# Attention of layer 0: the five blocks of queries in the order 1, 2, 0, 3, 4 instead of 0, 1, 2, 3, 4

## The chip, the cores and the metric

The kernel runs on one core of a Trainium2 chip. The metric is the device time of one execution in microseconds (us). Three executions of the kernel before took 2100.63, 2105.58 and 2110.71 us; their median is 2105.58. The profile comes from an execution of its own, which took 2108.86 us.

The core's engines are named as in the profile: PE is TensorE's matrix work and PEld its weight loads, DVE is VectorE, ACT is ScalarE, POOL is GpSimd, SP issues DMA transfers. A matrix instruction is a MATMUL; a transpose is one too (against the identity matrix, called `ca` in the rows). TensorE's granted clock is 2.4 GHz (shown as 1.00) or 1.2 GHz (0.50).

## The reference, cut to what matters

The program is one step of a two-layer network over 640 tokens: 128 of a prompt and 512 of a sample. In layer 0 two groups of heads work side by side on one input projection, and one output projection takes both results:

```python
def block_attention(q, k, v):            # 8 query heads, 2 key heads, 64 wide
    def one_block(qblk):                 # 128 queries
        s = jnp.einsum('bqkgd,bskd->bkgqs', qblk, k).astype(F32) * scale
        p = jax.nn.softmax(s, axis=-1).astype(v.dtype)
        return jnp.einsum('bkgqs,bskd->bqkgd', p, v)
    o = lax.map(one_block, qb)
...
attn = block_attention(q, keys, vals)    # prompt: its own 128 keys; sample: 128 cached + 512 own
y_f, hf = ssd_chunked(xs, ...)           # a scan in chunks of 128 tokens, forward
y_b, hb = ssd_chunked(xs[:, ::-1], ...)  # and backward
out = jnp.einsum('bte,ed->btd', jnp.concatenate([attn, y], axis=-1), w_out)
```

A block of queries needs nothing of another block. The prompt's one block (block 0) sees 128 keys; each of the sample's four (1 to 4) sees 640.

## The kernel before, in words

The tokens stand in five blocks of 128: block 0 is the prompt, 1 to 4 the sample. Keys, values and queries of all five lie in SBUF when the stage begins; nothing of the attention is loaded in it.

`attention(b)` works through the eight heads in pairs (0 and 4, 1 and 5, ...). For each head TensorE makes the scores in PSUM (`psS`, L728: for a long block two halves of 320 keys, each from a high and a low part of the keys, so four matmuls; for block 0 two matmuls of 128). VectorE takes the row maximum (`nm`, L731) and scales it (L732), ScalarE makes the exponentials (`pe`, L734), TensorE transposes them (`pT`, L739: five transposes, or one for block 0; the fifth goes into free columns of `psS`), ScalarE and VectorE copy them out (`pts`, L742 and L744), and after every second head TensorE multiplies both with the values (`po`, L751). At the end of a block the sums of all heads are inverted and spread (L755 to L763), and the result is split into a high and a low part for the output projection (`mh`, `ml`, L768 and L769). There are two PSUM tiles for scores and one for transposes.

`ssd()` is the scan. It first makes decay factors (`sums`, L781) and the states carried from chunk to chunk (`states`, two directions: GpSimd's product `xde` at L803, TensorE's L807, VectorE's updates of `hT` at L823 and L825), and then for each chunk of 128 tokens a chain over all engines (`chunk`: L843, L863 with exponentials at L865, L875, for chunks 1 to 4 L882, then a norm over the row on VectorE, and the transposes of L706 into `mh` and `ml`).

Both are Python generators. The loop at L910 to L915 takes one head of attention and one step of the scan in turn: 40 heads against 37 steps, so the scan ends with the last block. Below it a scheduler lays the instructions into one fixed order for each engine by priority (order of writing) and by its own estimate of when an engine is free; every engine then runs its list in that order and waits where an input isn't ready. So both the order of writing and the scheduler's estimate set what stands behind what.

Of the kernel before, what the change touches and what calls it, by code (L numbers as in the profile page):

```python
# [83 lines left out]
def build(tc, I, O):  # L84
    with ExitStack() as ctx:
        _build(ctx, tc, I, O)


def _build(ctx, tc, I, O):
# [358 lines left out]
    with l0st as st:  # L448
# [242 lines left out]
        with ExitStack() as s1:  # L691
# [208 lines left out]
            def ssd():  # L900
                sums()
                for d in range(2):
                    steps_of(0, d)
                yield from states(0)
                yield from states(1)
                for b in range(5):
                    yield from chunk(b)
                    yield

            other = ssd()  # L910
            for b in range(5):
                for _ in attention(b):
                    next(other, None)
            for _ in other:
# [1055 lines left out]
```

## Time and profile before

| what | number |
|---|---|
| runs | 2100.63, 2105.58, 2110.71 us; median 2105.58 |
| profiled execution | 2108.86 us |
| its span in the profile | 2107.0 us |
| TensorE busy in the span | 1940.9 us (92%) |
| VectorE, ScalarE, GpSimd busy | 1433.5, 941.8, 563.4 us (68%, 45%, 27%) |
| mean granted clock of TensorE | 0.942 |
| the attention stage | 200.65 to 377.03 us |

The span is what the profiler saw from the first to the last instruction; the time of the execution is 1.9 us longer. "Busy" of TensorE counts from the start of a matmul to its modelled end, so where matmuls follow each other the distance of their starts says what one costs. A granted clock of 0.50 doubles that distance. Idle time is given with what ended it: "[1.36 <-POOL xde L803]" reads: idle for 1.36 us, until GpSimd's instruction of line 803 that wrote `xde`.

### The profile page before, as it was taken

Reading aid. Unit: us, or ns where it says so; the run is one execution under the profiler, and the core shown is the slowest. Engines: PE = TensorE matmul, PEld = TensorE weight load, DVE = VectorE, ACT = ScalarE, POOL = GpSimd, SP = SyncE. Lnnn points to the kernel's source line nnn. Section 1 sums busy time; section 2 is a strip of 40 time slices with the busy share of each in tenths; the row PEclk is TensorE's granted clock in tenths of the full one; section 3 lists DMA queues with packets and bytes.
Section 4 is the critical chain, followed back from the end, with each engine's and each line's share of the span. In section 5 each row is a group of like instructions: output and inputs, shape, how many; then the busy total and the mean of one; then the engine's idle time right before and its main releaser. Section 6 shows DMA issues by size and latency. Waiting matters only on the chain. (4 is left out here: it accounts for less than half of the span.)

```text
span 2107.0 us, 42812 instructions
## 1 busy us (share of the span) xinstructions
PE 1940.9 (92%) x17625; PEld 1767.9 (84%) x17625; DVE 1433.5 (68%) x2597; ACT 941.8 (45%) x1742; POOL 563.4 (27%) x515
## 2 busy tenths in 40 slices
PE   7999989999999999989999897877789899999998
PEld 6888677989999999968676886766679799999998
DVE  4474676458675757678585839889966777666675
ACT  4332445344433524446665343444463535344351
POOL 2111232001343426031144123313321025243330
PEclk8999899999999999989999988878879999999999
DMA  9764000522342424332377634435344422323221
GB/s 293 224 202 113 9 1 1 170 91 81 110 141 81 149 62 131 121 119 66 118 234 247 207 101 129 120 86 147 93 148 125 121 80 81 101 64 97 61 91 51
DMA packets 256406, 245.71 MB, mean 117 GB/s; under 512 B 27849, under 2 KB 217298, under 8 KB 256084
## 3 DMA queue, kind: packets, MB, share of 16 engines
q1 hardware_dynamic: 233076, 208.87, 32.9%
q0 software_dynamic: 5856, 21.01, 3.1%
q10 hardware_dynamic: 17280, 13.11, 2.0%
q8 instruction: 138, 2.26, 0.4%
q14 instruction: 56, 0.46, 0.1%
HBM read 203.76 MB, written 39.19 MB: 115 GB/s over the span
## 5 line engine op out<-in xcount | busy, mean ns | idle before, releaser
L979 DVE TENSOR_TENSOR ol<-wr,oh 128x512 fp32r<-128x512 f32 x344 | 304.7, 902 | 103.9 <-ACT oh L978 96.0
L978 ACT CAST oh<-wr 128x512 fp32r<-128x512 f32 x344 | 211.2, 620 | 312.4 <-PE d L1130 176.1
L1130 PE MATMUL d<-hid,oh 128*128 128x320 f32 x1312 | 292.5, 311 | 3.6 <-DVE hid L1028 2.1
L1130 PEld LDWEIGHTS d<-hid,oh 128*128 128x128 f32 x1312 | 221.6, 189 | 5.1 <-DVE hid L1028 3.3
L1130 PE MATMUL d<-hid,ol 128*128 128x320 f32 x656 | 203.8, 311 | 0.0
L443 DVE SCALAR_TENSOR_TENSOR x<-d,mod,x 128x128 f32<-128x128 f32 (+2 forms) x204 | 77.3, 433 | 142.6 <-PE d L1130 116.3
L1000 POOL TENSOR_TENSOR g<-wr 128x512 f32<-128x512 f32 x36 | 49.4, 1372 | 459.1 <-DMA wr<-in_ffn_w_up_dram 315.0
L1130 PEld LDWEIGHTS d<-hid,ol 128*128 128x128 f32 x656 | 124.3, 189 | 0.0
L401 PE MATMUL d<-hh,wh 128*128 128x320 f32 (+1 forms) x464 | 118.7, 328 | 3.9 <-ACT at L1404 1.8
L401 PE MATMUL d<-hl,wh 128*128 128x320 f32 (+1 forms) x464 | 114.4, 319 | 2.7 <-POOL hl L436 2.7
L401 PE MATMUL d<-hh,wl 128*128 128x320 f32 (+1 forms) x464 | 113.5, 316 | 0.4 <-DVE wl L388 0.4
L388 DVE TENSOR_TENSOR wl<-wr,wh 128x1024 fp32r<-128x1024 f32 (+1 forms) x57 | 72.3, 1269 | 56.8 <-ACT wh L386 56.4
L386 ACT CAST wh<-wr 128x1024 fp32r<-128x1024 f32 (+1 forms) x57 | 58.7, 1034 | 102.6 <-PE d L401 64.9
L401 PEld LDWEIGHTS d<-hh,wh 128*128 128x128 f32 (+1 forms) x464 | 79.1, 190 | 16.5 <-ACT at L1404 3.9
L401 PEld LDWEIGHTS d<-hl,wh 128*128 128x128 f32 (+1 forms) x464 | 79.3, 190 | 7.1 <-POOL hl L436 5.4
L1027 ACT CAST hid<-e 128x320 fp32r<-128x320 f32 x88 | 40.5, 460 | 97.9 <-DVE e L1045 97.4
L401 PEld LDWEIGHTS d<-hh,wl 128*128 128x128 f32 (+1 forms) x464 | 79.8, 190 | 2.1 <-DVE wl L388 1.1
L1553 PE MATMUL pS<-ar,ta 64*128 64x128 f32 x640 | 58.6, 325 | 21.8 <-POOL uv L1621 10.2
L1003 POOL TENSOR_TENSOR wr<-wr 128x512 f32<-128x512 f32 x36 | 52.7, 1468 | 84.3 <-DVE ol L979 32.9
L1553 PEld LDWEIGHTS pS<-ar,ta 64*128 64x128 f32 x640 | 51.2, 227 | 28.4 <-POOL ar L1540 12.4
L1005 POOL TENSOR_TENSOR wr<-wr 128x512 f32<-128x512 f32 x36 | 54.0, 1512 | 65.3 <-DVE ol L979 64.3
L1581 DVE TENSOR_TENSOR xt__11678<-ta 128x31 f32<-128x31 f32 (+15 forms) x155 | 67.3, 434 | 4.4 <-POOL ta L1569 0.2
(637 smaller groups left out, 5957.3 us busy)
## 6 DMA issues: line engine op xcount, KB each, us to landing
wt<-in_mod_w_dram SPq DMA_DIRECT2D x80, 512.0 KB, 4.4
wr<-in_ffn_w_gate_dram SPq DMA_DIRECT2D x44, 512.0 KB, 4.7
wr<-in_ffn_w_up_dram SPq DMA_DIRECT2D x44, 512.0 KB, 5.0
wr<-in_ffn_w_down_dram SPq DMA_DIRECT2D x44, 512.0 KB, 4.5
ta<-kbd SPq DMA_DIRECT2D x10, 1024.0 KB, 6.9
ar<-rkd SPq DMA_DIRECT2D x20, 512.0 KB, 6.8
wr<-in_ab_w_in_dram SPq DMA_DIRECT2D x16, 512.0 KB, 8.0
wt<-in_mod_w_dram SPq DMA_DIRECT2D x6, 1024.0 KB, 10.5
```

Source lines behind the costliest of these rows:

```text
L386: S.copy(wh, wr)
L388: V.tensor_sub(wl, wr, wh.bitcast(F32))
L401: T.matmul(ps[b][0:cn, 0:320], w[:, k, 0:cn], a[:, t0:t1], start=(k == 0 and i == 0), stop=(k == w.shape[1] - 1 and i == 2))
L443: V.scalar_tensor_tensor(out=x[:, k, c0:c1], in0=ps[b][:, c0 - 320 * b:c1 - 320 * b], scalar=mod[:, layer, v, gcol + k:gcol + k + 1], in1= ...
L978: S.copy(hi, src)
L979: V.tensor_tensor(out=lo, in0=src, in1=hi.bitcast(F32), op=ALU.subtract)
L1000: E.tensor_tensor(out=g3, in0=a11, in1=a21, op=ALU.add)
L1003: E.tensor_tensor(out=a11, in0=a11, in1=a21, op=ALU.add)
L1005: E.tensor_tensor(out=a12, in0=a12, in1=a11, op=ALU.add)
L1130: T.matmul(bank[:, 0:c1 - c0], p, q, start=i == 0 and z == 0, stop=i == n - 1 and z == 2)
L1553: T.matmul(pS[i][:, m], bk[r, g4 * 4 + m, :], ar[r, g4 * 4 + m], start=True, stop=True)
L1581: V.tensor_tensor(out=tv, in0=nu[:, j + 1:32, j:j + 1].to_broadcast([128, n, j + 1]), in1=wu[:, j:j + 1, 0:j + 1].to_broadcast([128, n, j ...
```

## The change

The loop over the blocks of queries takes them in another order; nothing else is written differently.

```diff
             other = ssd()
-            for b in range(5):
+            for b in (1, 2, 0, 3, 4):
                 for _ in attention(b):
                     next(other, None)
```

The scan's steps keep their order and their turns. Before, the eight heads of block 0 alternate with the eight steps of `states`; now the heads of block 1 do, and block 0 comes third, in turns 17 to 24, beside the end of chunk 1 and the most of chunk 2 as they are written. The scheduler then orders each engine's list anew. GpSimd's list is the same as before, and so is everything behind this stage.

TensorE where the stage begins, before. `psS` are scores (kh and kl the high and low part of a key group, qs the queries), `pg` the scan's results, `pT` transposes, `po` the products with the values; the last number is the shape that an instruction writes, x4 that four stand in a row:

```order
L728 MATMUL psS<-kh_208,qs 128x128
L728 MATMUL psS<-kl_210,qs 128x128
L781 MATMUL pg_2176<-dta,cb__207 128x40 x4
L781 MATMUL pg_2176<-dta,ca 128x40 x2
L794 MATMUL pg_2193<-ca,h_2191 64x128 x4
L728 MATMUL psS<-kh_209,qs 128x128
L728 MATMUL psS<-kl_211,qs 128x128
L739 MATMUL pT<-ca,pe 128x128
L728 MATMUL psS<-kh_208,qs 128x128
L728 MATMUL psS<-kl_210,qs 128x128
L807 MATMUL pg_2202<-xde,btok 64x256 x2
L739 MATMUL pT<-ca,pe 128x128
```

And with the change, at the same place:

```order
L728 MATMUL psS<-kh_208,qs 128x320
L728 MATMUL psS<-kl_210,qs 128x320
L728 MATMUL psS<-kh_208,qs 128x320
L728 MATMUL psS<-kl_210,qs 128x320
L781 MATMUL pg_2183<-dta,cb__207 128x40 x4
L781 MATMUL pg_2183<-dta,ca 128x40 x2
L794 MATMUL pg_2200<-ca,h_2198 64x128 x4
L728 MATMUL psS<-kh_209,qs 128x320
L728 MATMUL psS<-kl_211,qs 128x320
L728 MATMUL psS<-kh_209,qs 128x320
L728 MATMUL psS<-kl_211,qs 128x320
L739 MATMUL pT<-ca,pe 128x128 x4
```

The first heads' scores are now of a long block (two halves of 320), and the first product of the scan's states (L807) stands behind five transposes instead of one.

VectorE at the same place, before (maximum, factor, the first carried state `hT`, and the decay factors `decg` and `dde` that GpSimd's first `xde` needs):

```order
L731 TENSOR_REDUCE nm<-psS 128x1
L732 TENSOR_SCALAR nm<-nm,rq 128x1
L796 COPY hT<-pg_2193 128x256
L731 TENSOR_REDUCE nm<-psS 128x1
L732 TENSOR_SCALAR nm<-nm,rq 128x1
L784 COPY decg<-ex 64x40 x2
L785 TENSOR_TENSOR dde<-ex,dtt 128x80
L823 TENSOR_TENSOR hT<-hT,decg 128x256
```

With the change:

```order
L731 TENSOR_REDUCE nm<-psS 128x1
L796 COPY hT<-pg_2200 128x256
L732 TENSOR_SCALAR nm<-nm,rq 128x1
L731 TENSOR_REDUCE nm<-psS 128x1
L784 COPY decg<-ex 64x40 x2
L785 TENSOR_TENSOR dde<-ex,dtt 128x80
L732 TENSOR_SCALAR nm<-nm,rq 128x1
L823 TENSOR_TENSOR hT<-hT,decg 128x256
```

The copy of `hT` now stands ahead of the first head's factor, and `dde` behind the second head's maximum only.

TensorE with the change behind the state products of chunk 1 (L882), where the short block now runs; these rows stand ahead of the chunk's transposes (L706):

```order
L728 MATMUL psS<-kh_208,qs 128x128
L728 MATMUL psS<-kl_210,qs 128x128
L882 MATMUL pg_2914<-hT,bc 128x256
L882 MATMUL pg_2915<-hT,bc 128x256
L739 MATMUL pT<-ca,pe 128x128
L728 MATMUL psS<-kh_209,qs 128x128
L728 MATMUL psS<-kl_211,qs 128x128
L751 MATMUL po<-pts,vt 64x128
L739 MATMUL pT<-ca,pe 128x128
L728 MATMUL psS<-kh_208,qs 128x128
L728 MATMUL psS<-kl_210,qs 128x128
L751 MATMUL po<-pts,vt 64x128
```

Before, the same place held heads of a long block:

```order
L728 MATMUL psS<-kh_208,qs 128x320
L728 MATMUL psS<-kl_210,qs 128x320
L728 MATMUL psS<-kh_208,qs 128x320
L728 MATMUL psS<-kl_210,qs 128x320
L882 MATMUL pg_2848<-hT,bc 128x256
L882 MATMUL pg_2849<-hT,bc 128x256
L739 MATMUL pT<-ca,pe 128x128 x4
L739 MATMUL psS<-ca,pe 128x128
L751 MATMUL po<-pts,vt 64x128 x9
L728 MATMUL psS<-kh_209,qs 128x320
L728 MATMUL psS<-kl_211,qs 128x320
L739 MATMUL pT<-ca,pe 128x128 x4
```

There short heads with 128 keys stand now, with one transpose each, where heads with 640 keys and five transposes stood.

## Rows read from the trace of the kernel before

**Rows 1.** Stretches: length, busy PE, PEld, DVE, ACT, POOL (count), granted clock, DMA.

```profile
200.65:228.18 27.53, 24.73 (x112) 14.23 (x110) 14.84 (x41) 8.91 (x27) 10.05 (x10) 0.59 0.20 54
228.18:254.50 26.32, 24.25 (x206) 20.18 (x205) 16.96 (x49) 14.47 (x33) 5.91 (x5) 0.98 0.00 1
254.50:282.50 28.00, 25.17 (x204) 20.33 (x204) 20.56 (x56) 14.84 (x34) 9.51 (x8) 1.00 0.01 1
282.50:312.50 30.00, 26.04 (x230) 21.43 (x224) 21.35 (x55) 14.27 (x33) 9.93 (x7) 1.00 0.01 1
312.50:340.05 27.55, 24.44 (x194) 19.66 (x193) 18.80 (x51) 13.52 (x29) 9.42 (x7) 1.00 0.00 1
340.05:365.97 25.92, 23.67 (x194) 19.38 (x193) 17.60 (x54) 14.33 (x32) 2.53 (x2) 1.00 0.00 1
```

**Rows 2.** The same view, shorter stretches at the stage's start and end.

```profile
203.00:204.00 1.00, 0.27 (x2) 0.13 (x2) 0.96 (x5) 0.99 (x4) 0.00 (x0) 1.00 0.52 153
205.00:206.00 1.00, 0.00 (x0) 0.00 (x0) 0.56 (x3) 0.06 (x1) 1.00 (x1) 0.73 0.88 231
206.00:207.00 1.00, 0.90 (x4) 0.29 (x4) 0.00 (x0) 0.00 (x0) 1.00 (x2) 0.50 0.80 231
229.00:230.00 1.00, 1.00 (x6) 0.80 (x6) 1.00 (x7) 0.58 (x2) 0.00 (x0) 0.82 0.00 0
364.00:366.00 2.00, 1.27 (x10) 0.79 (x9) 1.60 (x8) 1.30 (x3) 0.00 (x0) 0.97 0.00 0
366.00:368.00 2.00, 2.00 (x16) 1.67 (x16) 0.35 (x1) 0.46 (x2) 0.00 (x0) 0.50 0.00 0
```

**Rows 3.** Timeline of PE at full clock: start us, us, what was done.

```profile
255.05 0.66 PE L739 MATMUL pT<-ca,pe 128*128 128x128 f32 x4
255.57 0.39 PE L728 MATMUL psS<-kh,qs 128*128 128x320 f32 x1
256.33 0.49 PE L843 MATMUL pg<-bc 64*128 64x128 f32 x2
256.75 0.43 PE L751 MATMUL po<-pts,vt 128*64 128x128 f32 x2
257.11 0.41 PE L728 MATMUL psS<-kh,qs 128*128 128x320 f32 x1
...
348.29 1.30 PE L751 MATMUL po<-pts,vt 128*64 128x128 f32 x18
349.53 1.55 PE L875 MATMUL pg<-xdt,e 128*128 128x64 f32 x12
```

**Rows 4.** Timeline of PE in the stage's first part, at half clock.

```profile
206.10 1.12 PE L807 MATMUL pg<-xde,btok 128*64 128x256 f32 x4 [1.36 <-POOL xde L803]
207.15 0.48 PE L739 MATMUL pT<-ca,pe 128*128 128x128 f32 x1
207.56 0.69 PE L751 MATMUL po<-pts,vt 128*64 128x128 f32 x2
208.18 0.48 PE L728 MATMUL psS<-kh,qs 128*128 128x128 f32 x1
208.59 0.69 PE L751 MATMUL po<-pts,vt 128*64 128x128 f32 x2
...
226.81 0.64 PE L728 MATMUL psS<-kh,qs 128*128 128x320 f32 x1
```

**Rows 5.** Timeline of DVE where the stage begins.

```profile
201.81 1.23 DVE L388 TENSOR_TENSOR wl<-wr,wh 128x1024 fp32r<-128x1024 f32 x1 [0.17 <-ACT wh L386]
...
203.28 0.21 DVE L732 TENSOR_SCALAR nm<-nm,rq 128x1 f32<-128x1 f32 x1
203.41 0.41 DVE L796 COPY hT<-pg 128x256 f32<-128x256 f32 x1
```

**Rows 6.** Groups in the stage: shape, count, busy us, mean ns, idle before them.

```profile
L734 ACT ACTIVATE pe<-psS,nm,rq 128x640 f32<-128x640 f32 x32 | 28.3, 885 | 28.6 <-PE psS L728 18.4 <-DVE nm L732 4.9 <-DVE rq_w L121 2.5
...
L731 DVE TENSOR_REDUCE nm<-psS 128x1 f32<-128x640 f32 x32 | 26.2, 819 | 6.3 <-PE psS L728 6.3
```

## The prediction

> **What bounds the kernel now.** I read the page first, for the span (2107.0 us) and its row of the granted clock. The change touches one stage only, the attention of layer 0 with the scan that runs beside it, from 200.65 to 377.03 us; behind it the instructions are the same on every engine and in the same order. So I cut that stage with the windows view at the places where the scan passes from one part to the next: first the states (sums and carried states, up to the first matmul of L843), then the five chunks (each up to the transposes of L706) [rows 1]. What is to be seen: in the five chunk phases TensorE is busy 24.25, 25.17, 26.04, 24.44 and 23.67 us of 26.32, 28.00, 30.00, 27.55 and 25.92. That is 123.57 of 137.79, and 14.2 us idle; VectorE has 95.3 busy. TensorE is the engine that sets the pace there, at a full clock. The states phase is another thing: 27.53 us, 24.73 of them busy, but at a mean granted clock of 0.59. Taken at full clock its work is about 24.73 x 0.59 = 14.6 us. So some 12.9 us of this phase are idle time and half clock. The finer windows show how it came: TensorE is busy 0.27 us between 203 and 204 and not at all between 205 and 206, the granted clock falls to 0.50 (1.2 GHz) there and is back at 1.00 (2.4 GHz) only after 229 [rows 2]. All eight heads of block 0, the prompt's short one, run inside that stretch.
>
> **What the change moves.** Nothing is added or removed; the same instructions stand in another order, and GpSimd's order is unchanged. A head of a long block costs TensorE, by the distance of starts at full clock [rows 3]: five transposes 255.05 to 255.57, 0.52; the four score matmuls to 256.33, 0.76; the ten matmuls on the values, two heads together 0.36 + 1.24, so 0.80 a head. Sum 2.08 us. A head of the short block at half clock [rows 4]: transpose 0.41, score matmuls 2 x 0.41, values 0.62: 1.85, so 0.92 at full clock.
>
> Counted in TensorE's order, the states phase had 8 short heads and the score matmuls of one long head; it gets 7 long heads. The five chunk phases had 6, 6.75, 6, 6 and 6 long heads (in quarters, by score matmuls issued); now they have 8.75, then 1.25 and the 8 short ones, then 4, 3.75 and 7. What follows the last chunk's transposes is the same as before, with the same quarter head to go, so it costs the same.
>
> States phase: 14.6 - 8 x 0.92 - 0.76 + 7 x 2.08 = 21.0 us of work at full clock. On top come three terms. First, idle time at the start. VectorE is held by the weight split until about 203.04, then takes 0.82 for the first long maximum, 0.41 for a copy that now stands ahead of the factor, and 0.21 for the factor; ScalarE's exponential takes 0.89 [rows 5, 6]. So the first transpose can start near 205.5; TensorE has issued two heads' scores and the state sums by about 204.1 (with two short heads' it was done by 203.3: it is busy 0.27 us after 203 [rows 2]), which leaves 1.4 idle. Then the first state matmul waits for GpSimd's product, as it did for 1.36 us before [rows 4]; its input comes after the second long maximum, about 1 us later than before, but five transposes stand ahead of the wait: 1.0 idle. For the rest of the phase I take 1.5, half of a chunk phase's mean idle time (14.2/5 = 2.8). Together 3.9; between 2.4, the start alone, and 5.2 with a whole phase's. Second, the clock: the thin stretch at the start is still there, so I expect the fall still to happen near 206. But from about 207 on long heads follow each other. In the trace the clock came back within 3 us of the first long head's score matmuls (they begin at 226.81) [rows 2, 4]; if it does so again, some 3 us of busy time run at half clock, 1.5 lost. Bounds: 0 if it never falls, and about 18 if all work after the start runs at half clock. Sum: 21.0 + 3.9 + 1.5 = 26.4, against 27.53: a gain of 1.1.
>
> Chunk phases: 6 long heads leave (30.75 to 24.75), 8 short ones come: -6 x 2.08 + 8 x 0.92 = -5.1. Two terms stand against it, both in the phase of chunk 1, where the short heads now run. Its TensorE work becomes 25.17 - 5.5 x 2.08 + 8 x 0.92 = 21.1; with the smallest idle time of a phase (2.07) it could end in 23.2. But the chunk is a chain over all engines, and no chunk phase of the trace is shorter than 25.92, so between 0 and 2.7 us of it are idle beyond the usual: I take 1.5. And TensorE is thin again behind that chunk's state products, while VectorE does the row norm of the chunk. How the clock takes such a stretch can be seen at the end of the stage: with 1.27 of 2 us busy between 364 and 366 it falls to 0.50 [rows 2]. It came back soon there, since dense work followed. One such fall costs about half of 3 us of busy work, 1.5; the bounds are 0 and about 10, what the states phase lost (24.73 - 14.6 = 10.1). So the chunk phases change by -5.1 + 1.5 + 1.5 = -2.1.
>
> Total: -1.1 - 2.1 = -3.2. The profiled execution took 2108.86 us (span 2107.0), so 2105.7 on its base. The median of the three runs is 2105.58, 3.3 below it, and I state the time against the median: 2102.4.
>
> A rule that speaks against this change: the Trainium skill, "TensorE: Matmul & The Clock Gate", section "HAM oscillation — how this bites in real kernels", says that a loop whose bursts are parted by waits pays for the return of the clock again in every turn, and that it is better to keep the engine fed throughout. By it a thin stretch moved to the middle pays there a second time, on top of the one that the start still has; that is the second rival below, priced from rows.
>
> **Rivals.**
> *The clock holds in both places.* For it: with long heads TensorE has more to do in the first microseconds (eight long score matmuls instead of four short), and the thin stretch of chunk 1 has, by the windows, neighbours that are dense. Against it: the 2.4 us of idle time at the start follow from VectorE's order, not from the clock. Then the states phase takes 21.0 + 2.4 = 23.4 (-4.1), with the start's idle time alone, and the chunk phases -5.1 + 0.8, with half of the chain's idle time: -8.4, about 2097.
> *The half clock moves with the short block.* For it: the short heads ran at half clock for 24 us because they give TensorE too little, and they are as small in the middle. Against it: there they run beside a chunk's dense matmuls and not beside the states. The start still loses 1.5, and the middle loses 9 to 10 instead of 1.5: -3.2 + 8 = +5, about 2108 to 2111: no change that can be told.
> *The clock doesn't come back at the start, slower.* One mechanism, in the states phase: after the fall near 206 long heads at half clock wait often enough, for GpSimd's products and the one transpose bank, that the clock stays down until the chunk's matmuls. Price: 21.0 - 2.5 = 18.5 us of work at half clock, +18.5 in place of +1.5: -3.2 + 17 = +14, about 2117 to 2120. It decides from the point where the clock is still at 0.50 by the fourth long head (about 217). Against it: 229 to 230, where the very first long heads brought it back.
> That the change doesn't move the work is ruled out by the orders above: the long block stands first on TensorE and VectorE.
>
> **How the numbers follow.** The forecast has 0.55 (its own range 2098 to 2107), the clock that holds 0.20, the half clock in the middle 0.14, the slow start 0.11. I take 0.5%, about 10.5 us, as what a measurement tells from no change: the three runs span 2100.63 to 2110.71. Faster by more (below 2095.0) is the low half of the first rival and a rest of the forecast's tail: 0.15. Slower by more (above 2116.1) is nearly all of the third rival: 0.10. The rest, 0.75, is within. The range 2092 to 2113 holds the forecast, most of the first rival and the second, and leaves out the third and the far end of the first.
>
> **What would show it.** In the profile after: the states phase with 7 long heads in 25 to 28 us, its granted clock above 0.8 and no longer 0.59; a fall near 206 that ends before 213; the phase of chunk 1 shorter than 28.0 us, 23 to 26, with a dip of the clock of a few us behind its state products; chunk 0 and chunk 4 each longer than before by about two heads (4 to 6 us) and one head (2 us), chunk 3 shorter by about 4.5. Wrong would be a states phase at 0.6 again, or chunk phases whose sum doesn't fall below 137.8 us, which would mean that the chunks' chain and not TensorE set their length.

## The result, and the profile after

The changed kernel takes 2117.30 us (median of 6 runs, 2114.86 to 2119.52), the kernel before 2104.84 (6 runs, 2100.63 to 2110.71): a ratio of 1.0057, 95% interval [1.0043, 1.0071]. I forecast 2102.4 with a range of 2092 to 2113. The change makes the kernel slower, by 12.5 us, and the prediction was wrong in its sign.

The profiled execution has a span of 2117.2 us against 2107.0. The stage begins 0.36 us later and takes 10.8 us more; all that lies behind it takes 1 us less. These are its stretches, cut at the same places as [rows 1] and with the same columns (length, busy PE, PEld, DVE, ACT, POOL, granted clock, DMA): states, chunks 0 to 4, and what follows the last chunk's transposes.

```profile
201.01:226.59 25.58, 22.91 (x165) 16.17 (x163) 17.82 (x42) 11.44 (x21) 10.03 (x10) 0.87 0.22 58
226.59:260.30 33.71, 29.64 (x258) 24.87 (x259) 21.46 (x58) 17.58 (x39) 6.02 (x5) 1.00 0.00 1
260.30:289.30 29.00, 27.36 (x181) 21.21 (x177) 19.92 (x58) 13.12 (x42) 9.74 (x7) 0.79 0.00 1
289.30:318.20 28.90, 23.87 (x160) 18.80 (x158) 19.34 (x51) 12.49 (x30) 9.48 (x7) 0.85 0.00 1
318.20:350.45 32.25, 27.44 (x173) 22.19 (x172) 16.58 (x42) 9.80 (x22) 10.05 (x7) 0.79 0.00 1
350.45:377.59 27.14, 24.77 (x198) 20.32 (x198) 18.81 (x56) 15.01 (x34) 2.54 (x2) 1.00 0.01 2
377.59:388.19 10.60, 8.20 (x67) 6.55 (x65) 2.76 (x8) 3.41 (x8) 0.00 (x0) 0.76 0.66 230
```

Read each row in three parts: work (busy PE times clock: what the busy time would be at full clock), half clock (busy PE times one minus clock: what the lower clock adds) and idle (length less busy PE). The states phase did what was forecast: 25.58 us in place of 27.53, at a clock of 0.87 in place of 0.59. The five chunk phases grew from 137.8 to 151.0 us, and by their parts:

| five chunk phases, us | before | after | difference | forecast |
|---|---|---|---|---|
| work | 123.1 | 118.0 | -5.1 | -5.1 |
| idle | 14.2 | 17.9 | +3.7 | +1.5 |
| half clock | 0.5 | 15.1 | +14.6 | +1.5 |

The work left the chunk phases nearly as counted. (A row's mean clock is only a rough divider. With the busy time summed inside the half-clock stretches themselves, work comes to 122.9 and 116.6 us and half clock to 0.6 and 16.5; idle time is the same.) The clock took back about three times as much. Shorter stretches of the same view show where: TensorE runs at 1.2 GHz from about 277 to 294 us, from 315 to 322, from 332 to 339, and for 3 us from 346. Before, no chunk phase but the first microsecond of chunk 0 had any of that.

```profile
276.00:278.00 2.00, 1.17 (x6) 0.97 (x6) 1.93 (x6) 0.49 (x2) 0.79 (x2) 0.82 0.03 8
277.30:294.40 17.10, 16.97 (x66) 11.51 (x66) 9.05 (x39) 7.62 (x28) 3.57 (x3) 0.50 0.00 1
294.00:296.00 2.00, 2.00 (x18) 1.80 (x15) 1.23 (x4) 0.58 (x1) 0.00 (x0) 0.91 0.00 0
314.00:316.00 2.00, 0.12 (x1) 0.12 (x2) 1.79 (x12) 1.15 (x3) 0.00 (x0) 0.71 0.00 0
314.85:321.68 6.83, 5.80 (x31) 4.54 (x31) 3.49 (x17) 3.53 (x8) 1.04 (x1) 0.50 0.00 0
331.90:338.75 6.85, 6.85 (x40) 5.84 (x38) 0.69 (x1) 0.00 (x0) 2.04 (x2) 0.50 0.00 0
344.00:346.00 2.00, 1.43 (x7) 1.01 (x8) 1.76 (x13) 1.73 (x5) 0.00 (x0) 0.89 0.00 0
345.57:349.00 3.43, 3.41 (x13) 2.62 (x13) 1.05 (x7) 0.75 (x2) 0.00 (x0) 0.50 0.00 0
```

Half of the busy time of such a stretch is what its clock cost: 8.5, 2.9, 3.4 and 1.7 us, 16.5 together. The first of these stretches is the short heads'. TensorE's timeline reads there as it did in the states phase before [rows 4]: transposes, scores and values of a short head at half clock, 1.4 to 1.5 us from head to head.

```profile
280.38 0.48 PE L739 MATMUL pT<-ca,pe 128*128 128x128 f32 x1
280.51 0.46 PE L728 MATMUL psS<-kh,qs 128*128 128x128 f32 x1
280.76 0.41 PE L728 MATMUL psS<-kl,qs 128*128 128x128 f32 x1
281.21 0.69 PE L751 MATMUL po<-pts,vt 128*64 128x128 f32 x2
```

The other three have no short head near them. They stand in the phases of chunks 2 and 3, which have 4 and 3.75 long heads in TensorE's list where there were 6 and 6. Rows of the timeline from the norm of chunk 2 (the first row) and from chunk 3 show what TensorE does there (the brackets give idle time of the engine and what ended it; most rows between are left out):

```profile
315.88 1.12 PE L739 MATMUL pT<-ca,pe 128*128 128x128 f32 x4 [2.19 <-ACT pe L734]
...
324.91 0.68 DVE L866 TENSOR_TENSOR e<-e,gm 128x512 f32<-128x512 f32 x1
325.23 4.42 POOL L834 TENSOR_TENSOR am<-cb__207,dta 128x1024 f32<-128x1024 f32 x2 [5.74 <-PE pg L863]
325.81 4.99 DVE L866 TENSOR_TENSOR e<-e,gm 128x512 f32<-128x512 f32 x3
330.25 5.17 PE L875 MATMUL pg<-xdt,e 128*128 128x64 f32 x30 [1.39 <-DVE e L866]
335.46 0.69 DVE L876 TENSOR_TENSOR ys<-pg,ys 128x512 f32<-128x512 f32 x1 [4.13 <-PE pg L875]
340.62 0.82 DVE L731 TENSOR_REDUCE nm<-psS 128x1 f32<-128x640 f32 x1
342.08 0.69 DVE L891 TENSOR_TENSOR ys<-ys,zs 128x512 f32<-128x512 f32 x1 [0.63 <-POOL ys L888]
342.69 0.21 DVE L732 TENSOR_SCALAR nm<-nm,rq 128x1 f32<-128x1 f32 x1
342.81 0.63 ACT L894 ACTIVATE sc__3422<-ys 128x512 f32<-128x512 f32 x1 [14.57 <-DVE ys L891]
343.43 0.86 ACT L734 ACTIVATE pe<-psS,nm,rq 128x640 f32<-128x640 f32 x1
344.44 0.66 PE L739 MATMUL pT<-ca,pe 128*128 128x128 f32 x4 [3.28 <-ACT pe L734]
```

Two kinds of wait are seen. At 330.25 the y products (L875) wait 1.39 us for `e`; the clock falls behind it, and the thirty products take 5.17 us. At 315.88 and 344.44 the transposes of a head wait 2.19 and 3.28 us for its exponential (L734) while the chunk does its row norm, and the clock falls in the first of these waits and behind the second. The norm stands ahead of that head in two lists: VectorE has the head's maximum (L731) by 341.44, but then waits 0.63 us for GpSimd's sum and multiplies (L891) before it makes the head's factor (L732, 342.69), and ScalarE squares (L894) before the exponential. ScalarE's idle time of 14.57 us ahead of that square is not the length of this hold-up: until 340.62 VectorE hadn't begun the maximum of that head's scores, so for most of it there was no exponential to make. Before, ScalarE's list of this chunk had two heads' exponentials between the chunk's own last one (L865) and that square; now it has none. The groups of the stage show the same shift, against [rows 6]: the long exponentials cost the same (883 against 885 ns), but their idle time is now 11.4 us for VectorE's factor in place of 4.9, and 6.5 for scores in place of 18.4.

```profile
L734 ACT ACTIVATE pe<-psS,nm,rq 128x640 f32<-128x640 f32 x32 | 28.2, 883 | 22.4 <-DVE nm L732 11.4 <-PE psS L728 6.5 <-DVE rq_w L121 1.9
...
L731 DVE TENSOR_REDUCE nm<-psS 128x1 f32<-128x640 f32 x32 | 26.3, 821 | 8.6 <-PE psS L728 8.2
```

### The profile page after: what moved, and what is told of

It is laid out like the page before. It is cut to its first block, busy times and chain, and to the rows that moved or that the text cites. A ratio compares the mean times of both kernels' runs of the same rounds, so it can differ in the third digit from the quotient of the medians.

```text
span 2117.2 us, 42810 instructions
## 1 busy us (share of the span) xinstructions
PE 1948.1 (92%) x17625; PEld 1778.0 (84%) x17625; DVE 1437.9 (68%) x2597; ACT 941.1 (44%) x1742; POOL 565.7 (27%) x515
## 5 line engine op out<-in xcount | busy, mean ns | idle before, releaser
L978 ACT CAST oh<-wr 128x512 fp32r<-128x512 f32 x344 | 211.3, 620 | 310.3 <-PE d L1130 175.2
L1553 PEld LDWEIGHTS pS<-ar,ta 64*128 64x128 f32 x640 | 48.9, 216 | 30.7 <-POOL ar L1540 12.9
```

What stands on the lines that cost most here:

```text
L978: S.copy(hi, src)
L1553: T.matmul(pS[i][:, m], bk[r, g4 * 4 + m, :], ar[r, g4 * 4 + m], start=True, stop=True)
```

## The experiments

Two theories. *Short heads*: a run of short heads gives TensorE too little and the half clock moves with it. *Heads run ahead*: attention gets ahead of the scan (8.75 long heads beside chunk 0, short ones beside chunk 1), so chunks 2 and 3 keep four heads each, too few to cover the waits in the chunk's own steps. (The expectations of the first four runs set a *clock theory*, the first of these, against a *chain theory*: the scan's chain over all engines sets the length of a phase. The second theory came out of that one.) The table gathers all runs: long heads (+ short ones, s) beside chunks 0 to 4 in TensorE's list, then from the profile the stage (first scores to the last block's normalising product, L765), its idle time and half clock by the reading above, over seven stretches cut at each chunk's first L843 matmul (the before and after rows so differ a little from those above), and the ratio of times to the kernel before.

| kernel | heads beside chunks 0 to 4 | stage | idle | half clock | ratio [95% interval] |
|---|---|---|---|---|---|
| before | 6, 6.75, 6, 6, 6.25 | 177.1 | 19.2 | 13.4 | 1 |
| after | 8.75, 1.25+8s, 4, 3.75, 7.25 | 187.9 | 23.0 | 20.3 | 1.0057 [1.0043, 1.0071] |
| fill_before | as before | 174.4 | 19.1 | 6.3 | 0.9999 [0.9988, 1.0010] |
| fill_after | 8.75, 0.25+6s, 3.5+2s, 6.25, 6.25 | 187.9 | 20.9 | 16.6 | 1.0053 [1.0032, 1.0074] |
| o10234 | 2+8s, 4.5, 6.25, 6, 6.25 | 180.0 | 22.1 | 11.8 | 1.0012 [0.9997, 1.0028] |
| pace_after | 9, 2+8s, 4.75, 6.25, 3 | 175.2 | 20.2 | 10.9 | 1.0003 [0.9986, 1.0021] |
| lead_before | 8, 8, 4.5, 4, 6.5 | 202.4 | 25.8 | 29.9 | 1.0097 [1.0075, 1.0119] |
| spread | 6+2s, 7.75, 3.75+2s, 4.75+2s, 3.75 | 172.9 | 17.1 | 10.8 | 0.9983 [0.9970, 0.9995] |
| fill_mid | 8.75, 1.25+8s, 4.25, 4.25, 6.5 | 197.8 | 20.8 | 26.0 | 1.0112 [1.0090, 1.0133] |
| o12340 | 8.75, 6, 6, 4.25+1.5s, 6.5s | 170.1 | 18.8 | 7.8 | 0.9987 [0.9970, 1.0003] |
| amwait_after | 8, 1.75+8s, 4, 4.75, 6.5 | 204.1 | 30.4 | 30.0 | 1.0128 [1.0107, 1.0149] |
| amwait_before | 6, 6, 6.75, 4.75, 7.5 | 198.0 | 30.7 | 24.9 | 1.0110 [1.0092, 1.0128] |
| even | 7+1s, 4.5+1s, 4.5+2s, 5+1s, 5+1s | 189.9 | 18.7 | 21.7 | 1.0037 [1.0024, 1.0049] |
| amwait_even | 7+1s, 4.25+1s, 5.25+2s, 4.5+1s, 5+1s | 189.3 | 22.7 | 17.9 | 1.0071 [1.0054, 1.0089] |
| norm_after | 8.75, 1.25+8s, 4, 5, 6 | 184.3 | 23.2 | 16.4 | 1.0063 [1.0039, 1.0087] |
| even_last | 6.5, 6, 6, 6, 0.5+8s | 177.7 | 21.2 | 13.4 | 1.0014 [1.0000, 1.0028] |
| dveadd_after | 8.75, 0.75+8s, 3.5, 5, 7 | 197.2 | 21.0 | 30.6 | 1.0096 [1.0074, 1.0118] |
| dveadd_before | 6, 6, 6.5, 5.25, 7.25 | 171.7 | 18.0 | 5.8 | 0.9986 [0.9970, 1.0001] |

Before and after have 144.5 and 144.7 us of work by this reading, so all of the 10.8 us is half clock (+6.9) and idle time (+3.8). In spread, even and amwait_even the out-projection's first matmuls lie inside the stage. The stage is read from one execution of each kernel, the ratio from all of them: the profiled execution of even took 2119.22 us and that of o10234 2115.42, the longest of each (medians 2112.56 and 2107.42), so their stages may be longer than usual. From the stage's end to the end of the span the profiled executions take 1719.7 (lead_before) to 1733.3 us (fill_before). So stages are compared by their traces and times by the ratios.

**fill_before, fill_after.** Four dummy matmuls behind the scores of each short head:

```diff
+                    if b == 0:
+                        for f_ in range(4):
+                            T.matmul(psS[:, 1, 0:320], qs[:, h, 128:256], kh[h // 4][:, 128:448], start=f_ == 0, stop=f_ == 3)
```

> The kernel before, and in each of the eight heads of block 0 four matmuls of 320 columns more, into the unused half of that head's score tile; nobody reads them. Order otherwise unchanged. Clock theory (the short heads give TensorE too little, and the half clock is what costs): the states phase keeps 2.4 GHz or gets it back early, its work is 14.6 + 8 x 0.65 = 19.8 us at full clock with about 3 to 4 idle, so 23 to 25 us in place of 27.5: the kernel becomes 2 to 4 us faster although it does more, about 2101. Chain theory (the states' chain over GpSimd, TensorE and VectorE sets the pace, the clock is only a mark of it): 27.5 us or more, 0 to 5 us slower.

> The changed kernel with the same four matmuls more in each head of block 0, which stands third. Clock theory: the 17 us of half clock beside chunk 1 and 2 go, the added 5 us are paid back: 5 to 9 us faster than the changed kernel, 2108 to 2112. Chain theory: a chunk takes its 27 to 30 us whatever the clock: within 3 us of the changed kernel, 2114 to 2120, unless the scheduler spreads the long heads otherwise (by its order the phases get about 7, 8.75, 0 with 6 short, 4.25 with 2 short, 6.25 and 6.25 long heads; then the phase of chunk 3, which has 6.25 in place of 3.75, gets shorter than its 32 us by chain theory alone).

In the order of before the half clock at the start ended near 215 us instead of 229. The stage has 7.1 us of half clock less, 6.0 of them there, and the dummies' own work took 4.5. The states phase took 27.07 us (27.53 before), not the 23 to 25 of the clock theory, and the time didn't change. In the changed order they bought nothing: the clock was down from 277 to 297 all the same, and chunk 2 took 36.6 us at 0.70.

**o10234.** The short block second instead of third:

```diff
-            for b in (1, 2, 0, 3, 4):
+            for b in (1, 0, 2, 3, 4):
```

> Blocks in the order 1, 0, 2, 3, 4: long heads beside the states, the short block beside chunk 0. Long heads by phase: 7; 2 with 8 short; 4.5; 6.25; 6; 6.25. Clock theory: the states phase as in the changed kernel (25.6 us), the half clock once, for 15 to 20 us beside chunk 0, and then as before: 2108 to 2112. Chain theory: chunk 0 with 2 long and 8 short heads takes its 24 to 27 us as before with 6, chunk 1 with 4.5 takes 28, the others as before; so what the states phase gains (2 us) is all: 2103 to 2107.

The loss is nearly gone, though the short heads again stand in a run in the middle; the median, 2107.42, lies just between the two ranges. Beside them the clock was down from 250 to 264 us, but that fall stands at the end of a wait of 3.36 us for an exponential.

**pace_after.** The changed order, with the scan's steps given out by the weight of the heads:

```diff
-                for _ in attention(b):
-                    next(other, None)
+                for i_, _ in enumerate(attention(b)):
+                    for _ in range(int(b > 0 or i_ % 4 == 3) + (b > 1 and i_ == 3)):
+                        next(other, None)
```

> The changed order of blocks, but the scan takes a step only after every fourth short head, and two steps after the fourth head of blocks 2, 3 and 4, so that its 37 steps go with the long heads. Long heads by phase: 7; 9; 2 with 8 short; 4.75; 6.25; 3. Clock theory: the short heads still stand together beside chunk 1, half clock for 17 us: 2114 to 2119. Chain theory: chunk 3 with 6.25 heads in place of 3.75 no longer stalls (27.5 us in place of 32.3), but the last chunk has 3 heads in place of 7 and the end waits for its chain: 2110 to 2116.

With the same order of blocks the slowdown is gone (2105.36 us, below both ranges). The short heads still lose the clock (281 to 291 us, 10 us in place of 17), but chunks 2 and 3 lose it only for 3.4 us each. The edit changed both, so it doesn't say which of them counts for how much.

**lead_before.** The order of before, with no short head outside the states phase, but the scan held back in blocks 1 and 2 and doubled in block 3:

```diff
+            turns = (1,) * 8 + (1, 0, 1, 0, 1, 1, 0, 1) + (1, 1, 0, 1, 1, 0, 1, 1) + (2, 2, 2, 2, 2, 2, 1, 1) + (1,) * 8
...
-                for _ in attention(b):
-                    next(other, None)
+                for i_, _ in enumerate(attention(b)):
+                    for _ in range(turns[b * 8 + i_]):
+                        next(other, None)
```

> Order 0, 1, 2, 3, 4 as before, but the scan's steps are held back by some heads of blocks 1 and 2 and given out two at a time in block 3, so that the chunk phases have about 8, 8, 4.5, 4 and 6.5 long heads, as uneven as in the changed kernel, and no short head stands outside the states phase. Theory 'heads run ahead' (a chunk with only four long heads beside it leaves TensorE waiting in the chunk's own steps, which stretches the phase and lets the clock fall): chunks 2 and 3 not below 27.5 us each, with a mean granted clock under 0.90 in them, stage 183 to 187 us against 177.1, time 2111 to 2115. Theory 'short heads' (only the run of short heads in the middle costs): the clock stays above 0.97 in chunks 2 and 3, they shrink by about two heads to 24 to 26 us, chunks 0 and 1 grow by as much, stage 176 to 179, time 2103 to 2108.

This tells the theories apart: a loss comes without a short head outside the states phase, and a larger one than either theory gave (2125.85 us). These are the stretches of chunks 0 to 4; those of chunks 2 and 3 have 4.5 and 4 heads and are hardly shorter than those with 8 (33.3 and 32.4 us against 33.9 and 33.4).

```profile
228.87:262.81 33.94, 31.12 (x262) 25.74 (x261) 22.13 (x58) 17.92 (x42) 6.88 (x5) 0.93 0.00 1
262.81:296.18 33.37, 29.04 (x215) 23.45 (x214) 20.56 (x58) 15.69 (x36) 9.23 (x7) 0.95 0.01 1
296.18:329.52 33.34, 27.76 (x195) 22.88 (x194) 19.68 (x50) 12.20 (x31) 9.23 (x8) 0.85 0.00 1
329.52:361.87 32.35, 27.15 (x156) 20.67 (x155) 17.04 (x44) 9.79 (x22) 9.66 (x7) 0.75 0.00 1
361.87:390.50 28.63, 25.79 (x172) 21.23 (x171) 15.75 (x48) 11.55 (x27) 2.55 (x2) 0.80 0.00 1
```

TensorE's longest waits are of the same two kinds, for `e` and for an exponential at the row norm, and behind each of these the clock falls:

```profile
308.39 1.08 PE L875 MATMUL pg<-xdt,e 128*128 128x64 f32 x4 [2.22 <-DVE e L866]
324.30 0.66 PE L739 MATMUL pT<-ca,pe 128*128 128x128 f32 x4 [2.91 <-ACT pe L734]
...
340.22 4.53 PE L875 MATMUL pg<-xdt,e 128*128 128x64 f32 x30 [2.53 <-DVE e L866]
```

**spread.** The short heads in pairs in the middle of each long block (their sums on the values go to the free half of their score bank and are copied out; the carried states `hT` get 8 buffers in place of 9; the scan takes one step more between the two heads of a pair):

```diff
...
+            short = attention(0)
+            for b in range(1, 5):
+                for i_, _ in enumerate(attention(b)):
+                    next(other, None)
+                    if i_ == 3:
+                        next(short)
+                        next(other, None)
+                        next(short)
...
```

> The short block's heads in pairs in the middle of each long block (blocks 1, 2, 3, 4), their sums on the values in the free half of their score bank and copied out; no run of short heads anywhere. Theory 'short heads': with no run of them the clock loses only the fall at the start (about 3 us of busy time) and little at the end: 144 us of work at full clock, 19 us idle and 3 to 5 us by the clock, stage 166 to 170 us, time 2095 to 2099. Theory 'heads run ahead': the phases of chunks 2 to 4 have only 4 to 5 long heads beside them, so at least two of them show a clock under 0.90, and the stage takes 175 to 181 us, time 2103 to 2110.

Faster than the kernel before by 0.17% [0.05, 0.30], and so than both; less than the theory of short heads gave, and a little better than the other. Of chunks 2 to 4 one had a clock under 0.90 (0.88), where the second theory wanted two.

**fill_mid.** Dummies in the thin phases, in the changed order: four of 320 columns ahead of the transposes of each head of block 3, eight ahead of the y products of chunks 2 and 3.

```diff
+                    if b == 3:
+                        for f_ in range(4):
+                            T.matmul(pT[:, 0:320], qs[:, h, 128:256], kh[h // 4][:, 128:448], start=f_ == 0, stop=f_ == 3)
...
+                if b in (2, 3):
+                    for f_ in range(8):
+                        T.matmul(pY[:, 0:320], qs[:, 0, 128:256], kh[0][:, 128:448], start=f_ == 0, stop=f_ == 7)
```

> The changed order with dummy matmuls (their results are overwritten) where TensorE waits in chunks 2 and 3: four of 320 columns ahead of the transposes of each head of block 3, eight ahead of the y products of chunks 2 and 3, together 48, about 7 us at full clock. If the half clock is what makes these phases long: clock above 0.95 in chunks 2 and 3, the two together 53 to 57 us against 61.2, time 2110 to 2114. If the chain of waits through VectorE, ScalarE and GpSimd makes them long and the clock only follows: the two together 61 us or more, time 2117 to 2124.

Chunks 2 and 3 took 69.9 us together in place of 61 and the clock was no better:

```profile
287.60:323.76 36.16, 32.64 (x183) 26.01 (x182) 19.22 (x50) 12.27 (x29) 9.99 (x7) 0.74 0.00 1
323.76:357.51 33.75, 30.59 (x201) 25.50 (x200) 17.35 (x45) 11.26 (x26) 9.82 (x7) 0.80 0.00 1
```

No wait for an exponential over 1.3 us is left in these two phases. But TensorE still waits for `e` behind the dummies, 2.00 and 1.70 us (the y products are L881 here):

```profile
301.40 5.56 PE L881 MATMUL pg<-xdt,e 128*128 128x64 f32 x30 [2.00 <-DVE e L869]
...
334.34 4.48 PE L881 MATMUL pg<-xdt,e 128*128 128x64 f32 x30 [1.70 <-DVE e L869]
```

The clock falls behind each of these waits, and the time, 2127.72 us, is above both ranges. Here the dummies did not keep the clock up, and their work came on top.

**o12340.** The short block last:

```diff
-            for b in (1, 2, 0, 3, 4):
+            for b in (1, 2, 3, 4, 0):
```

> Order 1, 2, 3, 4, 0: the short block last, beside the last chunk. Chunks 0 to 3 have 8.75, 6, 6 and 4.25 long heads, the last chunk 6.5 short ones. Theory 'heads run ahead': only chunk 3 is thin, nothing comes behind the short heads but the out-projection: stage 168 to 173 us, time 2097 to 2101. Theory 'short heads': chunk 4 runs at half clock, 0.6 or below, and takes 26 us or more; stage 176 to 180, time 2104 to 2109.

The stage is the shortest of all, as the theory of heads that run ahead had it; the time, 2101.14, lies at the edge of its range, and its interval includes no change. The last chunk ran at 0.86, not at the 0.6 of the theory of short heads.

**amwait_after, amwait_before, even, amwait_even.** In the first two GpSimd's table for the next chunk takes the buffer of `e` and is written behind the y products, so it can't run beside VectorE's L866; even is built as spread, with single short heads after the second and sixth head of each long block and one step of the scan more after the fourth and eighth; the last has both.

```diff
-                am = ams[b, d] = wk.tile([128, 8, 128], F32, name="am", tag="am")
+                am = ams[b, d] = wk.tile([128, 8, 128], F32, name="am", tag="e")
...
-                    if b < 4:
-                        steps_of(b + 1, d)
                     yield
...
                 V.tensor_tensor(out=ys, in0=pY.rearrange("p (h d) -> p h d", h=8), in1=ys, op=ALU.add)
+                if b < 4:
+                    for d in range(2):
+                        steps_of(b + 1, d)
                 yield
```

> The changed order; GpSimd's decay table am of the next chunk takes the buffer of VectorE's product e, so it can only be written when the y products have read e, and no longer runs beside the product that makes e. Phases of 7, 8, 1.75 and 8 short, 4, 4.75, 6.5 heads, nearly as in the changed kernel. Theory 'the wait for e' (in a phase with few heads nothing on TensorE covers the wait of the y products for e, and the clock falls behind it): the three products in chunk 3 take 2.1 us and not 5.0, the wait of 1.4 us is gone, chunks 2 and 3 under 29 us each, time 2107 to 2112. Theory 'the wait at the row norm' (the heads' transposes that wait 2 to 3 us for an exponential queued behind the chunk's norm make the clock fall): those waits and the half clock behind them stay, time 2114 to 2119.

> The same shared buffer in the order 0, 1, 2, 3, 4. TensorE waited only 0.4 us in all for e there, so by both theories nothing to be gained: 2102 to 2107, unless the table now comes late for the next chunk (then chunk phases longer by 1 to 2 us each, 2107 to 2112).

> As the kernel with the short heads in pairs, but one short head at a time, after the second and the sixth head of each long block, so that the phases have about 6 + 2 short, 7 + 1, 4.5 + 1, 4.5 + 2, 5 + 1 and 5 + 1 short heads. If what costs is unevenness: no chunk phase over 31 us, fewer falls of the clock, 2095 to 2100. If phases with 4.5 long heads cost the clock whatever stands beside them: two of them at a clock under 0.90, 2101 to 2107.

> Both: short heads one at a time, and the shared buffer. If the wait for e is what makes thin phases lose the clock: 2092 to 2098; if the wait at the row norm does: as the even kernel alone, within 3 us of it.

L866 did become fast and the waits for `e` went. But the table now ran on GpSimd ahead of the sum (here L889) that the row norm waits for, and the heads' exponentials behind the norm came later still. VectorE's row and TensorE's two longest waits in amwait_after:

```profile
339.00 1.29 DVE L866 TENSOR_TENSOR e<-e,gm 128x512 f32<-128x512 f32 x2 [1.52 <-ACT e L865]
```

```profile
321.02 1.11 PE L739 MATMUL pT<-ca,pe 128*128 128x128 f32 x4 [6.76 <-ACT pe L734]
...
354.57 1.11 PE L739 MATMUL pT<-ca,pe 128*128 128x128 f32 x4 [5.14 <-ACT pe L734]
```

So this is no clean test of the wait for `e`; it shows that six heads a phase (amwait_before) are no cover for waits as long as these (up to 6.56 us there). All four medians, 2131.80, 2126.66, 2112.56 and 2120.07 us, lie above every range that was stated for them. And even was slower, not faster: with five long heads or fewer in four phases, chunk 3 took 43.5 us at a clock of 0.62 in its profiled execution.

**norm_after.** The row norm one step of the scan later:

```diff
+                yield
                 V.tensor_mul(ysf, ysf, zs[:, b, :])
...
                     yield from chunk(b)
-                    yield
```

> The changed order; the row norm of a chunk is written one step of the scan later, together with the next chunk's first step. In ScalarE's list of chunk 3 one more exponential stands ahead of the norm's square; chunk 2's list is as it was. Heads by phase 7, 8.75, 1.25 and 8 short, 4, 5, 6. Theory 'the wait at the row norm': the stall of 14.6 us of ScalarE in chunk 3 and TensorE's wait of 3.3 us are at most half of that, one fall of the clock less, chunk 3 29 us or less though it has one head more, time 2108 to 2113. Theory 'the wait for e': the wait of 1.4 us and the half clock behind it stay, chunk 3 32 us or more, time 2114 to 2119.

The fall at 346 us went, the wait fell from 3.28 to 2.27 us, and chunk 3 took 32.0 us with 1.25 heads more. But ScalarE's idle time was still 14.17 us, though an exponential and not the norm's square now stood behind it, and the wait for `e` (1.38 us) and the fall behind it stayed:

```profile
329.93 5.15 PE L875 MATMUL pg<-xdt,e 128*128 128x64 f32 x30 [1.38 <-DVE e L866]
...
342.09 0.89 ACT L734 ACTIVATE pe<-psS,nm,rq 128x640 f32<-128x640 f32 x1 [14.17 <-DVE nm L732]
...
343.12 0.66 PE L739 MATMUL pT<-ca,pe 128*128 128x128 f32 x4 [2.27 <-ACT pe L734]
```

The stage of the profiled execution (2115.92 us) is 3.6 us shorter, the time not: the interval covers that of the changed kernel. The median, 2118.76 us, lies in the range of the theory of the wait for `e`, and its other signs came too; the theory of the row norm was missed.

**dveadd_after, dveadd_before.** The two additions at L888 on VectorE:

```diff
-                        G.tensor_tensor(out=ys, in0=ys, in1=yo, op=ALU.add)
+                        V.tensor_tensor(out=ys, in0=ys, in1=yo, op=ALU.add)
```

> The changed order; the two additions of the state terms to ys run on VectorE (0.7 us each by its other products of 128x512) in place of GpSimd's 1.3 us and the hand-over between the engines. Heads by phase 7, 8.75, 0.75 and 8 short, 3.5, 5, 7. Theory 'the wait at the row norm': VectorE's waits of 3.6 us for the sum are gone, TensorE's waits of 2.2 and 3.3 us are at most 1.5 each, one fall of the clock less, time 2106 to 2112. Theory 'too few heads, wherever the waits stand': the waits move elsewhere in the phase and the half clock stays, time 2113 to 2120.

> The same in the order 0, 1, 2, 3, 4, where VectorE waited 2.0 us in all for that sum and the clock didn't fall behind it: no difference that can be told by either theory, 2102 to 2107.

In the changed order the 3.28 us wait at the norm of chunk 3 went, and the wait for `e` grew to 2.21 us; the wait at the norm of chunk 2 stayed (2.17). Chunks 2 and 3 took 35.6 and 37.7 us at 0.64 and 0.70. The waits moved, as the theory of too few heads had it, but the time, 2127.34 us, is above both ranges. In the order of before the same edit cost nothing.

```profile
321.00 0.66 PE L739 MATMUL pT<-ca,pe 128*128 128x128 f32 x4 [2.17 <-ACT pe L734]
...
338.73 6.36 PE L875 MATMUL pg<-xdt,e 128*128 128x64 f32 x30 [2.21 <-DVE e L866]
```

**even_last.** The order of o12340 with one extra step after the seventh head of block 1, so that chunks 0 to 3 have six heads each.

```diff
...
                     next(other, None)
+                    if (b, i_) in ((1, 6),):
+                        next(other, None)
```

> Order 1, 2, 3, 4, 0 with one extra step of the scan after the seventh head of block 1, so that the phases have 7, 6.5, 6, 6, 6 long heads and the last chunk the 8 short ones. Theory 'heads run ahead': chunks 0 to 3 as before the change (26 to 29 us each at a clock over 0.94), states 25 us, the last chunk and the rest 27 us: stage 161 to 167, time 2093 to 2097. Theory 'short heads': the last chunk at half clock takes 30 us or more with the rest, stage 170 to 175, time 2100 to 2105.

Missed: 2110.18 us, not 2093 to 2097 (nor the 2100 to 2105 of short heads). Chunks 0 to 2 took 31 to 33 us at 0.89 to 0.90 with 6 to 6.5 heads each, and at the row norm the transposes waited 1.97, 3.76 and 2.35 us. In the kernel before, the six heads stand otherwise against the norm, and the longest wait there was 1.85. The number of heads alone doesn't decide: o12340, with 8.75, 6 and 6, had no wait over 1.84. So the second theory, as it was stated, fails here: six heads beside a chunk can leave waits as long as four.

```profile
251.45 0.93 PE L739 MATMUL pT<-ca,pe 128*128 128x128 f32 x4 [1.97 <-ACT pe L734]
...
282.83 1.11 PE L739 MATMUL pT<-ca,pe 128*128 128x128 f32 x4 [3.76 <-ACT pe L734]
...
313.17 1.11 PE L739 MATMUL pT<-ca,pe 128*128 128x128 f32 x4 [2.35 <-ACT pe L734]
```

## Why the prediction was wrong

- *States phase, -1.1*: right in kind; -1.95 was measured. Its parts: work 19.9 (21.0 forecast), idle 2.7 (3.9), half clock 3.0 (1.5). These misses in part cancel each other, which is luck: the half clock there lasted 6.8 us and not 3. The fall came near 206 and ended before 213, and the first transposes started at 205.65 (205.5).
- *Chunk phases, work -5.1*: -5.1 by the rows' mean clocks, -6.3 by the half-clock stretches; right to about 1 us.
- *Chunk phases, idle +1.5*: +3.7, and in other places. I put it all into chunk 1, where idle time fell (2.83 to 1.64); chunk 0 has 2.0 us more, chunk 2 1.1 and chunk 3 1.7.
- *Chunk phases, one fall of the clock in the middle, +1.5 with bounds 0 and about 10*: this is the step that failed; +14.6 was measured. It had two faults. The fall beside the short heads lasted from 277 to 294 us and cost about 8.5 us: near the price of the second rival (9 to 10), to which I gave 0.14; "half of 3 us" a fall, read from the one at the stage's end, did not hold here. And I looked for falls only in chunk 1; the three later ones cost about 8 us more, and no rival had them. The phases of chunks 2 and 3, from which two heads each were to be taken, I wrote down as shorter ("chunk 3 shorter by about 4.5"; it grew by 4.7, and chunk 2 shrank by 1.1), as if a phase were its TensorE work plus a fixed idle time. What is taken from a phase is also the cover of its waits.
- The prediction named its own refutation: chunk phases whose sum doesn't fall "would mean that the chunks' chain and not TensorE set their length". This is half borne out. A phase with three heads can be short (pace_after's chunk 4, where GpSimd has no next table to make: 22.7 us at full clock), so the chain is no fixed floor of 25.9; but in lead_before thin phases stretch, without a short head, by waits and half clock to nearly the length of phases with twice the heads.
- The third rival, that gave the right time (2117 to 2120), had the wrong place: the clock came back at the start as forecast. That its number fits is chance.

The rule of the Trainium skill that I weighed, in "TensorE: Matmul & The Clock Gate", section "HAM oscillation — how this bites in real kernels", was on the right side: the clock fell four times in the chunk phases. Its own case is a loop that waits for DMA; the waits here were for other engines.

Shown: the work of the stage is unchanged (144.5 and 144.7 us); heads that run ahead of the scan make a loss without short heads (lead_before); another pacing in the same order takes the loss away (pace_after). That too few heads are left beside a chunk is the likely account, but argued: even_last lost the clock with six. Not settled: how much of the loss is the short heads' own stretch, about half of the half clock; which of the two waits in a thin phase would have to go; and how much the half clock costs apart from the waits that bring it. The edits at one wait (amwait, dveadd) made another longer, and the one that shortened a wait (norm) left the other as it was and didn't change the time.

## What to carry to other kernels

Where one stream of work covers the waits of another, moving work between phases isn't priced by its busy time alone: count what is left beside each phase and look which waits it covered. After a change of order compare not only how much stands in each engine's list, but which instruction stands behind a waiting one. Read a phase as work, half clock and idle: here the first term was right to about 1 us, and nearly the whole miss lay in the other two.

## What the runs showed of the hardware

TensorE's clock fell behind single waits within otherwise dense work: in the changed kernel and in lead_before, in or just behind every one of their seven waits of 1.99 to 3.28 us in the chunk phases. It isn't a plain rule: a wait of 2.27 us in norm_after and one of 2.36 in even_last had no fall. At 1.85 us both are seen at the same place, the norm of chunk 2: the kernel before had no fall there, while fill_before, o10234 and dveadd_before had one of 3.4 us. The fall at 332 us in the changed kernel came 1.7 us behind a wait of only 1.39. Beside the short heads the clock stayed at 1.2 GHz for 17.1 us, of which the row shows TensorE busy for 16.97.

VectorE's L866 took 0.68 us where it began ahead of GpSimd's L834 (324.91) and 2.08 us where L834 was already running (325.81, the first of the three); with L834 moved away, two took 1.29. This is not new with the change: before, L866 took 1.84 to 2.23 us beside L834 in chunks 1 to 3. The Trainium skill, "SBUF — State Buffer", section "SBUF: two separate sides", says that a VectorE instruction with two operands in SBUF and a GpSimd instruction that reads it take turns at a shared port; the rows agree.
